# An encoder block on one core: later row sums in the first block, reordered attention work, one sum of the down projection on another engine

## The chip, the cores and the metric

One core of a Trainium2 chip runs the whole kernel. The metric is device time in microseconds of one execution; the median of three runs is given. The core has five engines that work side by side, each with its own in-order queue of instructions: TensorE (PE, with its weight loads PEld), VectorE (DVE), ScalarE (ACT), GpSimd (POOL) and SyncE (SP), which here only starts transfers. They wait for each other by semaphores. SBUF is the on-chip memory of 128 partitions; PSUM has eight banks, into which PE accumulates.

## The reference

One layer of a bidirectional encoder over 512 tokens of width 2048, in float32:

```
h = RMSNorm(x) * g_mix
qA|kA|vA|qB|kB|vB = h @ W_in                  # widths 1024,256,256,1024,1024,1024
A = grouped-query attention, 8 heads of 128 on 2 k/v heads; q, k RMS-normalised per head,
    then 2-D axial rotary (row and column of the token in a grid 64 wide)
B = 8 heads, three dilated windows (128,1),(512,4),(2048,16) merged by their softmax sums;
    partial rotary on the first 32 of 128 dims
x = x + concat(RMSNorm(A), RMSNorm(B)) @ W_out
x = x + (silu(gate) * up) @ W_down,  gate|up = (RMSNorm(x) * g_ffn) @ W_gate_up    # 5632 each
out = RMSNorm(x) * g_final
```

## The kernel before, in words

**Precision.** Every large product is made of three fp32r matmuls (`mm3`, lines 133 to 135): each operand is split into hi (an ACT copy that rounds, `split_hi`, L221 and L223) and lo (DVE: the operand less hi, `split_lo`, L229 and L231), and PE sums hi*hi, hi*lo and lo*hi.

**Units.** The work is a list of units, in the order of PE. A standard unit (`Std`) multiplies 256 rows of a weight by 512 columns in two parts and is planned at 5.44 us (`STD_US`); a wide unit (`Wides`) is one 512-row step of one of seven products (m1 to m7) from which a 2 by 2 block product is put together, planned at 2.72 us (`WIDE_US`). Some of the seven need a sum or difference of weight blocks first: `weights` (L297 for the early blocks, L1072 in down) makes it on DVE, `between` (L1081) makes a second one.

**Order.** Nothing is reordered by a scheduler: the program's order is each engine's order. The loop at the end of the kernel (from L1344) goes through the units; `prepare(n)` starts loads on SP as far ahead as `load_ahead` says, then issues hi splits for up to four units ahead (8.2 us for wide units, 11 for standard ones) and lo splits one unit behind the hi splits. Weights live in a few buffers that are free again when hi and lo are made; the split pairs live in four buffers (`twin`). Functions that `hook(n, f)` leaves with unit n are issued after its matmuls. Two side lists (`side` for attention heads, `side2` for rope, tables and K) are emptied a little after every six matmuls of a standard unit (`tick`, `pump`) at `RATE_B`, `RATE_A` and `RATE_2` entries per unit and row block.

**Stages.** Units 0 to 7 make k and v of mixer A. Meanwhile x arrives in column form (`load_pair`), is scaled by its gain (`x_scale`, L344), split (`x_hi` L347, `x_lo` L350) and summed for the seven products (`x_sums`: L356 and L357 on GpSimd, L360 on DVE, L362 and L364). Rows of x come a second time in row form (`load_rows_in`, L385, through GpSimd's queue) and are squared and summed on ACT (`square_rows`, L388); `make_r1` turns the sums into 1/rms per token, `r1`, after unit 12. Results carry the factor r1 when they leave PSUM: `post_kvA` stores k and v of mixer A, `x_block` the products of three blocks of 28 wide units (v of B; q and k of B twice), in which `snap` copies a product (L463) and `add` adds another to it (L470).

Units 92 to 107 (`qa_chunk`) make q of mixer A and units 108 to 123 (`out_chunk`, kind B) the first half of the output projection. Between their matmuls lies attention: for each head `tq` and `tk` transpose q and k on PE and split them, `score` multiplies and takes the maximum (L685, L681) and the exponential (L687, L682), `weigh` divides by the sum (GpSimd L695, for the last block DVE L693), `pt` transposes and splits the probabilities (L124, L125), `pv` multiplies with v. `fin` splits the result o (hi L127, lo L128), squares it (L724, after the lo) and adds the square to a running sum (GpSimd L733). `push_norm_rope` puts five steps for a row block of q or k on `side2`: squares and 1/rms (`first`, L543), the part with sin on GpSimd (`turned`, L554), the part with cos on DVE (`straight`, L560, in place), their sum (`both`, L563), and the norm (`scaled`, GpSimd L566). `turn_k` transposes K of mixer A.

Then out_chunk A (units 124 to 139) finishes the output projection; `h_side` brings the new x into column form, with its lo halves on DVE (L939). Eleven blocks of 28 wide units make gate and up (`gate_up_block`), and `Down` multiplies by W_down in three passes: m1 with m7 eight units behind it, m6 with m4, m5 with m2, then m3. Each pass goes over 22 pairs of row blocks. In the first, m7 of a pair needs b = c - b (L1072), its hi and lo, and home = b + a (L1081), which m6 reads in the second pass. The left operand comes back from memory in chunks (`chunk`, lo on L1109). `spill_out` adds finished products to memory through GpSimd's queue (L1154).

Of the kernel before, what the change touches and what calls it, by code (L numbers as in the profile page):

```python
# [53 lines left out]
RATE_B, RATE_A, RATE_2 = 3.2, 3.2, 2.6  # L54
# [7 lines left out]
def encoder_block(ctx, tc, x, w_in, g_q_a, g_k_a, w_out, w_gate_up, w_down, g_final,  # L62
# [315 lines left out]
    ROW_AT = ((2, 6, 5), (3, 3, 6), (5, 6, 7), (6, 3, 8), (6, 2, 9), (7, 0, 10), (8, 1, 11), (9, 2, 12))  # L378
    x_rows_in = {}

    def load_rows_in(n):
        t, h = divmod(n, 2)
        at = ROW_AT[n][1]
        x_rows_in[n] = work_at(1024 * at, 1024) if at < 6 else early_a[:, 3].rearrange("p s c -> p (s c)")
        nc.gpsimd.dma_start(x_rows_in[n], x[0, t * P:(t + 1) * P, h * (D // 2):(h + 1) * (D // 2)])  # L385
# [46 lines left out]
    def post_kvA(t, ps):  # L432
        k0 = work_at((0, 512, 2048, 2560)[t], 512)
        nc.scalar.activation(k0, ps[t], AF.Copy, scale=r1["r"][:, t:t + 1])
# [3 lines left out]
    KV_UNITS = in_chunk(1024, lambda t, ps: hook(KP + 4, lambda: post_kvA(t, ps)), None)  # L438
# [6 lines left out]
    def x_block(lo0, lo1, dst0, dst1, late=0):  # L445
# [12 lines left out]
        def snap(form, half, name):  # L458
            def go():
                turns["stage"] += 1  # L460
                d = st[name] = stage[turns["stage"] % 3]
                for t in range(2):
                    nc.scalar.activation(d[:, t], box.bank_of(form)[t], AF.Copy, scale=r(half, t))  # L463
            return go

        def add(form, half, name):
            def go():
                d = st[name]
                for t in range(2):
                    nc.vector.scalar_tensor_tensor(d[:, t], box.bank_of(form)[t], r(half, t), d[:, t],  # L470
                                                   op0=OP.mult, op1=OP.add)
            return go

        def store(dst, half, name):
            return lambda: nc.gpsimd.dma_start(dst[:, 2 * half:2 * half + 2], st[name])
        box.after("m1", late, snap("m1", 0, "c11"))
        box.after("m7", 0, snap("m7", 1, "c22"))
        box.after("m6", 0, snap("m6", 1, "c21"))
        box.after("m2", 1, add("m2", 0, "c11"))
        box.after("m2", 2, store(dst0, 0, "c11"))  # L480
        box.after("m5", 1, add("m5", 1, "c22"))
        box.after("m5", 2, store(dst1, 1, "c22"))
        box.after("m4", 1, add("m4", 1, "c21"))
        box.after("m4", 2, store(dst0, 1, "c21"))
# [50 lines left out]
    def push_norm_rope(q0, dst, t, nh, name):  # L535
# [23 lines left out]
        def straight():  # L559
            nc.vector.tensor_tensor(q3, q3, tabs[name][0][:, t, :][:, None, :].to_broadcast([P, nh, HD]), op=OP.mult)  # L560

        def both():
            nc.vector.tensor_tensor(q0, q0, st["tmp"][:, :w], op=OP.add)  # L563
# [4 lines left out]
        side2.extend((first, turned, straight, both, scaled))  # L568
# [4 lines left out]
    def load_kvA():  # L573
        kvr["t"] = slot("kvr", F32, (P, NT, 512))
        nc.sync.dma_start(kvr["t"], kv_dram)

    kv_split = once("kvs", [P, 8, 512], F32R)

    def push_kvA():
# [12 lines left out]
        side2.append(split_v)  # L592
        kvr["turn"] = [lambda: turn_k(0), lambda: turn_k(1)]
# [3 lines left out]
    def post_qA(j, t, ps):  # L597
# [6 lines left out]
        if j == 0 and t == NT - 1:  # L604
# [844 lines left out]
```

## Time and profile before

| | us |
|---|---|
| median of 3 runs | 2001.19 (2000.93 to 2002.81) |
| the profiled execution | 2002.41 |
| its span, first to last instruction | 2000.6 |
| PE busy | 1971.6 |
| DVE busy | 1490.2 |
| ACT busy | 990.7 |
| POOL busy | 204.0 |
| mean granted clock of PE | 0.997 of full speed |

The span is what the profiler records of the program itself; the execution's time has some 2 us around it. A busy time is the union of an engine's instructions. Matmuls follow each other faster than each one lasts, so PE can be busy without a gap and still not be at its peak. The granted clock is a share of the full 2.4 GHz; 0.50 is 1.2 GHz.

### The profile page before, as it was taken

The page shows a single profiled execution, that of the slowest core. Times are in us where ns is not written, and L with a number is a line of the kernel's source. Part 1 is how long each engine was busy: PE and PEld are TensorE (multiplying, and loading weights), DVE is VectorE, ACT ScalarE, POOL GpSimd, SP SyncE. Part 2 cuts the span into 40 slices and gives each one's busy share as a digit, 9 for nine tenths or more (in the row PEclk, how much of TensorE's full clock was granted, in tenths as well). Part 3 has the DMA queues.
Part 4 walks back from the last instruction along what each step waited for, and adds up shares of the span by engine and source line. Part 5 has one row for each costly group of instructions (what it writes and reads, how often), then busy time and mean ns, then how long its engine had stood idle before and what let it go on. Part 6 is the DMA issues. An engine that isn't in the chain of part 4 may idle for free.

```text
span 2000.6 us, 23772 instructions
## 1 busy us (share of the span) xinstructions
PE 1971.6 (99%) x8932; PEld 1619.6 (81%) x8932; DVE 1490.2 (74%) x1731; ACT 990.7 (50%) x1262; POOL 204.0 (10%) x237
## 2 busy tenths in 40 slices
PE   9999999999999999999999999999999999999998
PEld 6788888777888888888888888888888887888886
DVE  6777666776654687777777877787778799788776
ACT  7644435554544554454444544444544545455464
POOL 3100014654220000000000000000000001002000
PEclk9999999999999999999999999999999999999999
DMA  6785684242334656657558567466475997479855
GB/s 234 256 278 178 202 275 140 95 136 76 129 103 150 228 171 230 216 165 265 177 199 271 174 218 259 159 230 229 156 264 190 341 363 233 161 243 339 284 179 176
DMA packets 219092, 418.67 MB, mean 209 GB/s; under 512 B 13664, under 2 KB 40032, under 8 KB 218720
## 3 DMA queue, kind: packets, MB, share of 16 engines
q1 hardware_dynamic: 210176, 389.86, 58.2%
q0 software_dynamic: 8656, 27.27, 4.4%
q8 instruction: 70, 1.15, 0.2%
q14 instruction: 46, 0.38, 0.1%
q10 hardware_dynamic: 144, 0.02, 0.0%
HBM read 369.65 MB, written 47.45 MB: 208 GB/s over the span
## 4 chain that ended last, share of the span: by engine, by line
PE 64%; DVE 2%; DMA 1%; issue 1%; ACT 1%; ACTq 0%; POOLq 0%; SPq 0%; POOL 0%; DVEq 0%
PE zc L133 8%; PE zc L135 8%; PE zc L134 8%; PE yc L134 4%; PE yc L135 4%; PE yc L133 4%; PE zd L134 4%; PE zd L135 4%; PE zd L133 4%; PE yd L135 3%; PE yd L133 3%; PE yd L134 3%; PE xc L133 2%; PE xc L134 2%; PE xc L135 2%; PE at L1005 1%
## 5 line engine op out<-in xcount | busy, mean ns | idle before, releaser
L231 DVE TENSOR_TENSOR twin<-whole,twin 128x1024 fp32r<-128x1024 f32 x172 | 214.1, 1246 | 101.6 <-ACT twin L223 101.3
L223 ACT ACTIVATE twin<-st1b 128x1024 fp32r<-128x1024 f32 x172 | 182.7, 1062 | 193.8 <-PE zc L135 66.5
L133 PE MATMUL zc<-twin,arena 128*128 128x512 f32 x704 | 277.1, 394 | 0.0
L135 PE MATMUL zc<-twin,arena 128*128 128x512 f32 x704 | 274.5, 390 | 0.0
L134 PE MATMUL zc<-twin,arena 128*128 128x512 f32 x704 | 274.1, 389 | 0.0
L223 ACT ACTIVATE twin<-whole 128x1024 fp32r<-128x1024 f32 x172 | 181.8, 1057 | 155.3 <-PE yc L135 74.0
L231 DVE TENSOR_TENSOR twin<-st1b,twin 128x1024 fp32r<-128x1024 f32 x172 | 209.9, 1221 | 33.2 <-ACT twin L223 32.6
L223 ACT ACTIVATE twin<-st1a 128x1024 fp32r<-128x1024 f32 x128 | 135.8, 1062 | 184.7 <-PE xc L135 58.2
L231 DVE TENSOR_TENSOR twin<-st1a,twin 128x1024 fp32r<-128x1024 f32 x128 | 156.4, 1223 | 69.9 <-ACT twin L223 64.9
L135 PEld LDWEIGHTS zc<-twin,arena 128*128 128x128 f32 x704 | 132.1, 188 | 28.1
L133 PEld LDWEIGHTS zc<-twin,arena 128*128 128x128 f32 x704 | 132.2, 188 | 27.0
L134 PEld LDWEIGHTS zc<-twin,arena 128*128 128x128 f32 x704 | 132.3, 188 | 26.3
L134 PE MATMUL yc<-twin,arena 128*128 128x512 f32 x352 | 137.2, 390 | 0.7 <-DVE twin L231 0.7
L133 PE MATMUL yc<-twin,arena 128*128 128x512 f32 x352 | 137.9, 392 | 0.0
L135 PE MATMUL yc<-twin,arena 128*128 128x512 f32 x352 | 137.1, 389 | 0.0
L134 PE MATMUL zd<-twin,form 128*128 128x512 f32 x348 | 135.5, 389 | 0.1
L133 PE MATMUL zd<-twin,form 128*128 128x512 f32 x348 | 135.6, 390 | 0.0
L135 PE MATMUL zd<-twin,form 128*128 128x512 f32 x348 | 135.4, 389 | 0.0
L1154 POOL DMA_DIRECT2D x1d<-ev x16 | 14.0, 873 | 1073.5 <-ACT ev L1153 1058.9
L134 PE MATMUL yd<-twin,form 128*128 128x512 f32 (+1 forms) x272 | 105.3, 387 | 1.6 <-DVE twin L231 1.6
L135 PE MATMUL yd<-twin,form 128*128 128x512 f32 (+1 forms) x272 | 105.1, 386 | 0.1
L133 PE MATMUL yd<-twin,form 128*128 128x512 f32 (+1 forms) x272 | 105.0, 386 | 0.0
(285 smaller groups left out, 4355.8 us busy)
## 6 DMA issues: line engine op xcount, KB each, us to landing
whole<-in_w_gate_up_dram SPq DMA_DIRECT2D x165, 512.0 KB, 5.1
whole<-in_w_in_dram SPq DMA_DIRECT2D x80, 512.0 KB, 4.6
st<-in_w_gate_up_dram SPq DMA_DIRECT2D x55, 512.0 KB, 3.9
st1a<-in_w_down_dram SPq DMA_DIRECT2D x48, 512.0 KB, 7.0
st1b<-in_w_down_dram SPq DMA_DIRECT2D x48, 512.0 KB, 8.5
st1a<-in_w_gate_up_dram SPq DMA_DIRECT2D x44, 512.0 KB, 7.3
st1b<-in_w_gate_up_dram SPq DMA_DIRECT2D x44, 512.0 KB, 6.5
forms<-pair SPq DMA_DIRECT2D x22, 896.0 KB, 6.7
```

The lines of the kernel that those rows point to most:

```text
L133: nc.tensor.matmul(dst, ah, bh, start=start, stop=False, skip_group_check=chained)
L134: nc.tensor.matmul(dst, ah, bl, start=False, stop=False, skip_group_check=chained)
L135: nc.tensor.matmul(dst, al, bh, start=False, stop=stop, skip_group_check=chained)
L223: nc.scalar.activation(self.pair[:, :, 0], self.src, AF.Copy)
L231: nc.vector.tensor_tensor(self.pair[:, :, 1], self.src, f32(self.pair[:, :, 0]), op=OP.subtract)
L1005: nc.tensor.transpose(ps[:, n * P:(n + 1) * P], src, ident)
L1154: nc.gpsimd.dma_start(x1_dram[2 * cb + j, row], e, accum_op=OP.add)
```

## The change

Four groups of edits:

- The rows of x are loaded after units 7 to 20 in place of 2 to 9, and squared at units 10 to 23 in place of 5 to 12; r1 is there from unit 23 on. `post_kvA` stores k and v without the factor, after units 8 to 11; `scale_kvA` applies it on ACT when they come back. The V block copies and adds its products without the factor and scales them on ACT ahead of the store (`store`), at later units. In units 0 to 7, and where the rate is 1.5 (out_chunk A), the lo splits are issued as far ahead as the hi splits. In units 0 and 1 `x_scale` comes ahead of a part of `prepare`.
- In `fin` the square of o is issued between hi and lo.
- The rope's part with cos is written to a buffer of its own ("rc"), with an empty step ahead of the sum; `RATE_2` goes from 2.6 to 3.2; the two `turn_k` come right after the rope of k.
- home = b + a (`between`), and in the last two steps of `h_side` the lo half of three forms, go from DVE to GpSimd.

```diff
--- before.py
+++ after.py
@@ -51,7 +51,7 @@
 CHUNK = 4
 ORDER = ("m1", "m4", "m5", "m3", "m2", "m7", "m6")
 X_AT = {"m1": (0, 1), "m4": (0, 2), "m2": (0, 3), "m5": (1, 0), "m6": (1, 1), "m7": (1, 2), "m3": (1, 3)}
-RATE_B, RATE_A, RATE_2 = 3.2, 3.2, 2.6
+RATE_B, RATE_A, RATE_2 = 3.2, 3.2, 3.2
 
 
 def f32(ap):
@@ -375,13 +375,11 @@
         return w[:, 0, lo:lo + P], w[:, 1, lo:lo + P]
 
     r1 = {}
-    ROW_AT = ((2, 6, 5), (3, 3, 6), (5, 6, 7), (6, 3, 8), (6, 2, 9), (7, 0, 10), (8, 1, 11), (9, 2, 12))
+    ROW_AT = ((7, 2, 10), (10, 2, 13), (13, 2, 16), (14, 0, 17), (16, 2, 19), (17, 0, 20), (19, 2, 22), (20, 0, 23))
     x_rows_in = {}
-
     def load_rows_in(n):
         t, h = divmod(n, 2)
-        at = ROW_AT[n][1]
-        x_rows_in[n] = work_at(1024 * at, 1024) if at < 6 else early_a[:, 3].rearrange("p s c -> p (s c)")
+        x_rows_in[n] = work_at(1024 * ROW_AT[n][1], 1024)
         nc.gpsimd.dma_start(x_rows_in[n], x[0, t * P:(t + 1) * P, h * (D // 2):(h + 1) * (D // 2)])
 
     def square_rows(n):
@@ -430,12 +428,12 @@
         return std_chunk(w_in, 0, lo, KP, mm, group, **kw)
 
     def post_kvA(t, ps):
-        k0 = work_at((0, 512, 2048, 2560)[t], 512)
-        nc.scalar.activation(k0, ps[t], AF.Copy, scale=r1["r"][:, t:t + 1])
+        k0 = work_at((1024, 1536, 0, 512)[t], 512)
+        nc.scalar.activation(k0, ps[t], AF.Copy)
         nc.gpsimd.dma_start(kv_dram[:, t], k0)
 
     QB, KB, VB = 1536, 2560, 3584
-    KV_UNITS = in_chunk(1024, lambda t, ps: hook(KP + 4, lambda: post_kvA(t, ps)), None)
+    KV_UNITS = in_chunk(1024, lambda t, ps: hook(KP + t, lambda: post_kvA(t, ps)), None)
     KV_UNITS[0].quick = KV_UNITS[0].raws[0].halves = True
     for n, u in enumerate(KV_UNITS):
         u.load_ahead = 20.0
@@ -460,28 +458,39 @@
                 turns["stage"] += 1
                 d = st[name] = stage[turns["stage"] % 3]
                 for t in range(2):
-                    nc.scalar.activation(d[:, t], box.bank_of(form)[t], AF.Copy, scale=r(half, t))
+                    if late and form != "m3":
+                        nc.scalar.activation(d[:, t], box.bank_of(form)[t], AF.Copy)
+                    else:
+                        nc.scalar.activation(d[:, t], box.bank_of(form)[t], AF.Copy, scale=r(half, t))
             return go
 
         def add(form, half, name):
             def go():
                 d = st[name]
                 for t in range(2):
-                    nc.vector.scalar_tensor_tensor(d[:, t], box.bank_of(form)[t], r(half, t), d[:, t],
-                                                   op0=OP.mult, op1=OP.add)
+                    if late:
+                        nc.vector.tensor_tensor(d[:, t], box.bank_of(form)[t], d[:, t], op=OP.add)
+                    else:
+                        nc.vector.scalar_tensor_tensor(d[:, t], box.bank_of(form)[t], r(half, t), d[:, t],
+                                                       op0=OP.mult, op1=OP.add)
             return go
 
         def store(dst, half, name):
-            return lambda: nc.gpsimd.dma_start(dst[:, 2 * half:2 * half + 2], st[name])
-        box.after("m1", late, snap("m1", 0, "c11"))
-        box.after("m7", 0, snap("m7", 1, "c22"))
-        box.after("m6", 0, snap("m6", 1, "c21"))
+            def go():
+                if late and name != "c12":
+                    for t in range(2):
+                        nc.scalar.activation(st[name][:, t], st[name][:, t], AF.Copy, scale=r(half, t))
+                nc.gpsimd.dma_start(dst[:, 2 * half:2 * half + 2], st[name])
+            return go
+        box.after("m1", 2 * late, snap("m1", 0, "c11"))
+        box.after("m7", 8 * late, snap("m7", 1, "c22"))
+        box.after("m6", 3 * late, snap("m6", 1, "c21"))
         box.after("m2", 1, add("m2", 0, "c11"))
-        box.after("m2", 2, store(dst0, 0, "c11"))
+        box.after("m2", 2 + late, store(dst0, 0, "c11"))
         box.after("m5", 1, add("m5", 1, "c22"))
-        box.after("m5", 2, store(dst1, 1, "c22"))
+        box.after("m5", 2 + late, store(dst1, 1, "c22"))
         box.after("m4", 1, add("m4", 1, "c21"))
-        box.after("m4", 2, store(dst0, 1, "c21"))
+        box.after("m4", 2 + late, store(dst0, 1, "c21"))
         box.after("m3", 0, snap("m3", 0, "c12"))
         box.after("m3", 1, store(dst1, 0, "c12"))
         return box
@@ -557,15 +566,17 @@
         q3 = q0.rearrange("p (h d) -> p h d", h=nh)
 
         def straight():
-            nc.vector.tensor_tensor(q3, q3, tabs[name][0][:, t, :][:, None, :].to_broadcast([P, nh, HD]), op=OP.mult)
+            st["cos"] = slot("rc")
+            c3 = st["cos"][:, :w].rearrange("p (h d) -> p h d", h=nh)
+            nc.vector.tensor_tensor(c3, q3, tabs[name][0][:, t, :][:, None, :].to_broadcast([P, nh, HD]), op=OP.mult)
 
         def both():
-            nc.vector.tensor_tensor(q0, q0, st["tmp"][:, :w], op=OP.add)
+            nc.vector.tensor_tensor(q0, st["cos"][:, :w], st["tmp"][:, :w], op=OP.add)
 
         def scaled():
             nc.gpsimd.tensor_tensor(dst.rearrange("p (h d) -> p h d", h=nh), q3,
                                     st["rs"][:, :, None].to_broadcast([P, nh, HD]), op=OP.mult)
-        side2.extend((first, turned, straight, both, scaled))
+        side2.extend((first, turned, straight, lambda: None, both, scaled))
 
     qA, kTA, vA = {}, {}, {}
     kvr = {}
@@ -573,6 +584,9 @@
     def load_kvA():
         kvr["t"] = slot("kvr", F32, (P, NT, 512))
         nc.sync.dma_start(kvr["t"], kv_dram)
+
+    def scale_kvA(t):
+        nc.scalar.activation(kvr["t"][:, t], kvr["t"][:, t], AF.Copy, scale=r1["r"][:, t:t + 1])
 
     kv_split = once("kvs", [P, 8, 512], F32R)
 
@@ -589,8 +603,7 @@
         def split_v():
             vA["v"] = split(kvr["t"][:, :, 256:], "vA", None, [kv_split[:, 4 + 2 * n:6 + 2 * n].rearrange(
                 "p a (b c) -> p (a b) c", b=2) for n in range(2)])
-        side2.append(split_v)
-        kvr["turn"] = [lambda: turn_k(0), lambda: turn_k(1)]
+        side2.extend((lambda: None, lambda: turn_k(0), split_v, lambda: turn_k(1)))
 
     q_rows = {}
 
@@ -601,8 +614,6 @@
         nc.scalar.activation(q0, ps[t], AF.Copy, scale=r1["r"][:, t:t + 1])
         push_norm_rope(q0, q0, t, 4, "q")
         side2.append(lambda: qA.__setitem__((j, t), q0))
-        if j == 0 and t == NT - 1:
-            side2.extend(kvr["turn"])
 
     pairB = {}
 
@@ -719,9 +730,10 @@
             sq = slot("sq") if self.h else misc[:, 2 + "BA".index(self.kind)]
             if last:
                 nc.scalar.activation(sq, self.o, AF.Square)
-            split(self.o, "oS", go[:, k:k + 1], (o[:, 0], o[:, 1]))
+            nc.scalar.activation(o[:, 0], self.o, AF.Copy, scale=go[:, k:k + 1])
             if not last:
                 nc.scalar.activation(sq, self.o, AF.Square)
+            nc.vector.scalar_tensor_tensor(o[:, 1], self.o, go[:, k:k + 1], f32(o[:, 0]), op0=OP.mult, op1=OP.subtract)
             if spill:
                 nc.gpsimd.dma_start(o_dram[self.h], o)
                 spilled.add(self.h)
@@ -801,6 +813,8 @@
     hook(n + 2, load_tables)
     hook(n + 3, push_tables)
     hook(n + 4, load_kvA)
+    for t in range(NT):
+        hook(n + 5 + t // 2, lambda t=t: scale_kvA(t))
     hook(n + 6, push_kvA)
     qa_chunk(1)
 
@@ -936,7 +950,7 @@
                 if half == 2:
                     nc.scalar.activation(hi, src, AF.Copy)
                 if half == 3 or not apart:
-                    nc.vector.tensor_tensor(lo, src, f32(hi), op=OP.subtract)
+                    (nc.gpsimd if apart and a else nc.vector).tensor_tensor(lo, src, f32(hi), op=OP.subtract)
         if half == (3 if apart else 2):
             hf[i] = True
 
@@ -1078,7 +1092,7 @@
         def between(self, form, q):
             if form == "m7":
                 a = self.home[q].t
-                nc.vector.tensor_tensor(a, self.raws[form, q]["b"].t, a, op=OP.add)
+                nc.gpsimd.tensor_tensor(a, self.raws[form, q]["b"].t, a, op=OP.add)
 
         def chunks(self):
             uses = {}
@@ -1292,17 +1306,17 @@
                     raw.load()
             done["load"] += 1
 
-    def prepare(n):
+    def prepare(n, most=4):
         load_raws(n)
         while done["side"] < len(units) and at[done["side"]] <= at[n] + SIDE_AHEAD:
             for v in units[done["side"]].side_in:
                 v.load()
             done["side"] += 1
-        while done["hi"] < min(len(units), n + 4) and at[done["hi"]] <= at[n] + units[done["hi"]].ahead:
+        while done["hi"] < min(len(units), n + most) and at[done["hi"]] <= at[n] + units[done["hi"]].ahead:
             load_raws(n)
             units[done["hi"]].split_hi()
             done["hi"] += 1
-            while done["lo"] < done["hi"] - 1:
+            while done["lo"] < done["hi"] - (n >= KP and units[n].rate != 1.5):
                 units[done["lo"]].split_lo()
                 done["lo"] += 1
         while done["lo"] <= n:
@@ -1358,14 +1372,17 @@
                 x_lo(n + 1)
             if 0 < n < KP - 2:
                 load_pair(n + 2)
-        for k, (first, _, at_unit) in enumerate(ROW_AT):
+        for k, (_, _, at_unit) in enumerate(ROW_AT):
             if n == at_unit:
                 square_rows(k)
         if n == ROW_AT[-1][2]:
             make_r1()
+        if n == 0:
+            prepare(n, 2)
+            x_scale(0)
+        elif n == 1:
+            x_scale(1)
         prepare(n)
-        if n < 2:
-            x_scale(n)
         for j in range(u.parts):
             u.mm(j)
             if j == 0 and n < KP:
```

## Rows read from the trace of the kernel before

**Rows 1.** What PE waited for, whole span: us in total, times, longest.
```profile
PE pj L134 <- DVE twin L231: 4.5, 4, 2.6
PE sc L133 <- DVE pTl L125: 4.4, 6, 1.7
PE o L133 <- ACT p L682: 1.7, 1, 1.7
PE sc L133 <- DVE xrows L855: 1.7, 1, 1.7
...
PE yc L134 <- DVE twin L231: 0.7, 1, 0.7
...
PE pw L134 <- DVE twin L231: 0.4, 1, 0.4
```

**Rows 2.** Windows by stage: length, then busy us of PE, PEld, DVE, ACT, POOL.
```profile
5.39:58.60 53.21, 48.72 (x192) 38.56 (x193) 38.13 (x37) 39.78 (x51) 21.67 (x23) 0.97 0.73 259
58.60:310.00 251.40, 251.40 (x1122) 208.09 (x1122) 178.59 (x174) 119.76 (x137) 25.82 (x37) 1.00 0.69 229
310.00:502.00 192.00, 181.50 (x882) 143.81 (x881) 135.90 (x327) 93.34 (x178) 97.41 (x110) 0.99 0.34 110
...
630.00:740.00 110.00, 108.71 (x507) 88.87 (x506) 76.57 (x98) 61.93 (x94) 1.92 (x1) 1.00 0.55 188
...
1584.90:1686.50 101.60, 99.93 (x438) 81.56 (x436) 99.65 (x90) 49.41 (x52) 3.55 (x4) 1.00 0.91 316
```

**Rows 3.** Windows of low clock; the seventh figure is PE's granted clock.
```profile
51.50:54.92 3.42, 3.04 (x7) 2.46 (x8) 3.42 (x4) 2.77 (x4) 1.44 (x2) 0.50 1.01 393
...
454.28:457.69 3.41, 3.41 (x11) 2.83 (x10) 2.26 (x4) 2.25 (x5) 2.10 (x2) 0.50 0.03 7
```

**Rows 4.** Line L388, squares of rows: ns min/median/max, first and last start.
```profile
L388 ACT ACTIVATE early_work<-early_work x6: 1041/1043/1061, 46.2 to 69.7; 128x1024 f32<-128x1024 f32 x6
```

**Rows 5.** Line L385, loads of rows, from issue to landing.
```profile
DMA to landing us min/median/max: 4.3/5.2/7.5
```

**Rows 6.** What ACT waited for at L724, 310 to 502 us.
```profile
ACT sq L724 <- DVE oS L128: 11.1, 5, 3.4
...
ACT misc L724 <- DVE oS L128: 2.0, 1, 2.0
```

**Rows 7.** What DVE waited for at L560, 310 to 502 us.
```profile
DVE qA L560 <- POOL ra L554: 10.7, 6, 2.6
...
DVE kvr L560 <- POOL ra L554: 2.9, 2, 1.8
```

**Rows 8.** Line L939, lo halves of the forms, 630 to 740 us.
```profile
L939 DVE TENSOR_TENSOR arena<-pair,arena x16: 949/1085/1227, 642.8 to 728.3; 128x1024 fp32r<-128x1024 f32 x8, 128x768 fp32r<-128x768 f32 x8
```

**Rows 9.** Line L1081 (22 in all): ns min/median/max, first and last start.
```profile
L1081 DVE TENSOR_TENSOR home<-st1a,home x8: 1219/1220/1222, 1588.3 to 1675.9; 128x1024 f32<-128x1024 f32 x8
```

**Rows 10.** Time line of DVE near 1680 us: start, duration.
```profile
1679.97 1.22 DVE L1081 TENSOR_TENSOR home<-st1b,home 128x1024 f32<-128x1024 f32 x1
1681.11 1.22 DVE L231 TENSOR_TENSOR twin<-st1b,twin 128x1024 fp32r<-128x1024 f32 x1
```

**Rows 11.** Time line of PE there; in brackets the idle time before.
```profile
1682.38 0.50 PE L134 MATMUL yd<-twin,form 128*128 128x512 f32 x1 [1.02 <-DVE twin L231]
```

**Rows 12.** Time line of DVE, 49 to 54 us.
```profile
49.47 0.68 DVE L360 TENSOR_TENSOR early_work<-early_work 128x512 f32<-128x512 f32 x1
50.08 1.75 DVE L231 TENSOR_TENSOR twin<-whole,twin 128x1024 fp32r<-128x1024 f32 x1
```

**Rows 13.** Time line of POOL, 49 to 54 us.
```profile
49.64 1.10 POOL L356 TENSOR_TENSOR early_work<-early_work 128x256 f32<-128x256 f32 x1 [0.42 <-DVE xsum L364]
50.82 1.59 POOL L357 TENSOR_TENSOR early_work<-early_work 128x256 f32<-128x256 f32 x1
```

**Rows 14.** Time line of DVE, 343 to 346 us.
```profile
343.15 1.22 DVE L231 TENSOR_TENSOR twin<-whole,twin 128x1024 fp32r<-128x1024 f32 x1
```

**Rows 15.** Time line of POOL, 343 to 346 us.
```profile
344.24 1.31 POOL L733 TENSOR_TENSOR misc<-misc,sq 128x512 f32<-128x512 f32 x1
```

## The prediction

> **What bounds the kernel now.** I read the list of what TensorE (PE) waited for first, then the busy times by stage, and only then the lists and time lines of the engines that feed it. The reader should see in [rows 1] that every large wait of PE is for VectorE (DVE) or ScalarE (ACT), none for a transfer, and in [rows 2] that the waits lie in four stretches. The rest is full: from 58.6 to 310 us PE is busy 251.40 of 251.40. The first block of the input projection idles 53.21 - 48.72 = 4.5 us, attention 192.00 - 181.50 = 10.5, the end of the output projection 110.00 - 108.71 = 1.3, the first pass of down 101.60 - 99.93 = 1.7. No matmul is added or taken away, so only these idle times, and new ones, can move the end. Twice an idle spell is followed by about 3.4 us at the lower clock, 0.50 [rows 3]: behind the stall at 49 us and behind that at 451 us. PE was busy there 3.04 of 3.42 and 3.41 of 3.41 us, at half pace, so about 1.7 us is lost each time. That makes 4.5 + 1.7 = 6.2 us to be had in the first block and 10.5 + 1.7 = 12.2 in attention.
>
> **The first block and the rows of x.** Eight squares of 1.04 us [rows 4] leave ACT in units 5 to 12, with their eight half-megabyte loads on GpSimd's queue, and the lo halves are issued a unit earlier on DVE. PE's four waits there, 4.5 us, are all for a lo (L231) [rows 1], which stands on DVE behind the lo of x, and that behind ACT. One unit earlier is 5.44 us in the plan (STD_US), twice the longest wait, 2.6. I take all 6.2 us. The squares land in units 10 to 23, inside the stretch where PE is full and ACT busy 119.76 of 251.40 [rows 2]. Each load has about three units (3 x 2.72 = 8.2 us) less the unit by which ACT runs ahead, 5.4 us at least, and landed in 4.3 to 7.5 us [rows 5]. A late one stops ACT for up to 2 us, behind it the hi halves of weights that are three units ahead: hidden, and if that cover went, 8 x 2 = 16 us. The four k/v stores and the three stores of the V block wait on the same queue and feed nothing before attention. The scaling moved behind r1 adds six ACT passes over 128x512 in the same full stretch; half of a 1.04 us pass each up to a whole one, 3 to 6 us on an engine with 130 us free: nothing.
>
> **Attention.** The square of o reads the PSUM bank that DVE's lo reads, and today it waits for that lo: ACT stood 11.1 + 2.0 us and two smaller times for it [rows 6], with the next hi of the probabilities behind it in ACT's queue. Ahead of the lo it waits for nothing, and the lo is up to 0.6 us later. The rope in place makes DVE's product with cos wait for GpSimd, which still reads the same q: 10.7 + 2.9 us [rows 7], with scores' maxima and lo halves queued behind. Out of place, only the sum needs GpSimd, three entries of the side list later instead of one. Side entries come 3.2/2.6 = 1.23 times as fast, but a rope has six instead of five: the same pace, nothing. The scores that waited for lo halves (4.4 us), for the maximum through the exponential (1.7) and for the residual row (1.7), and the low clock behind the second (1.7), are what late DVE work costs: 9.5 of 12.2. New are four ACT passes that scale k and v (2 to 4 us by the 1.04 of [rows 4], on an engine busy 93.34 of 192.00), for half a microsecond; and both K transposes come 2 entries behind the last GpSimd product that they read, where they came behind four more ropes. I take 9 us, between 0 (late work that only moves) and 12.2.
>
> **The output projection.** With the lo not held back, the 0.4 us wait at pw goes [rows 1]. But at its end two lo halves of 128x768 (0.95 us on DVE [rows 8]) go to GpSimd; by the working below they hold DVE 1.8 us, and the second stands just ahead of the 0.7 us wait at yc: +0.8. Together +0.4.
>
> **One sum of down on GpSimd.** The additions home = b + a (L1081) of 22 pairs, 1.22 us on DVE [rows 9], go to GpSimd. In the tail DVE starts an operation every 1681.11 - 1679.97 = 1.14 us [rows 10], and that is what it gets back for each. DVE is the engine with no room there: busy 99.65 of 101.60 [rows 2], and PE waited 1.02 us for its lo at 1682.38 [rows 11]. So whatever these operations do to DVE reaches the end one for one, and giving 22 x 1.14 = 25 us away sounds right. The trace speaks against it. At 49 us GpSimd adds beside DVE, and the two take turns: DVE's L360 ends at 49.47 + 0.68 = 50.15, GpSimd's L356, issued at 49.64, ends at 50.74, 0.59 after it; DVE's L231, issued at 50.08, ends at 51.83, 1.09 after that; GpSimd's L357, issued at 50.82, ends at 52.41, 0.58 after that [rows 12, 13]. DVE's operation took 1.75 instead of 1.22. So 128x256 holds DVE for 0.58 us. For 128x512: DVE's L231 ends at 343.15 + 1.22 = 344.37 [rows 14], L733, issued 344.24, at 345.55 [rows 15]: 1.18. The slope is 0.60 per 256 columns, so 128x1024, which no row shows, holds 0.58 + 3 x 0.60 = 2.38 us. DVE in down runs only operations with two inputs in SBUF, the kind that lost its turn at 50 us. Each moved sum thus costs 2.38 - 1.14 = 1.24 us in place of a gain: 22 x 1.24 = 27.3, less DVE's idle time 101.60 - 99.65 = 2.0, less the last sum's 2.4, whose end PE need not await: +23 us. Bounds: with no turns DVE has 25 us spare and the 1.7 us of waits vanish, -1.7; with two 128x512 additions whole, 2 x 1.31 = 2.62, it is 22 x 1.48 - 2 = +31. I take the row, because the operations on both sides are of its kind. PE would stand nearly half of the last nine units, and may see the low clock; since it then waits for DVE anyway I add nothing.
>
> The Trainium skill, SBUF — State Buffer, section "Who interferes with whom", says that a DVE instruction with two SBUF inputs and a GpSimd instruction that reads SBUF block each other for the whole instruction. The trace agrees, with 1.75 us for 1.22. The GPSIMD Engine Reference of the Trainium skill, "Elementwise — side-by-side cycle accounting", gives 4497 ns for an addition of 2048 columns; half, an estimate of 2.25 us, would make 22 x 1.11 - 4.4 = +20, and no row here shows it.
>
> **The sum.** The profiled execution took 2002.41 us (span 2000.6 and 1.8 around it), 1.2 above the median of 2001.19. 2002.4 - 6.2 - 9 + 0.4 + 23 = 2010.6; less the 1.2, 2009.4, and I say 2009.
>
> **Rivals.** *The sum hides beside DVE.* GpSimd then works in time in which DVE is not using the shared path, DVE drops to three quarters, the waits of down go: 2001.2 - 6.2 - 9 + 0.4 - 1.7 = 1985, faster. For it: GpSimd is idle through down but for a few issues (3.55 us [rows 2]). Against it: DVE has only 2 us without such an operation, and every overlap I followed took turns. It decides where the hold falls below 1.14 + (14.8 + 4.4)/22 = 2.0 us. Perfetto Trace Analysis of the Trainium skill, "Optimizing Scalar/DVE Operations", holds that with DVE saturated moving work, even to GpSimd, may make sense, and warns of the shared port for that pair; the first half is this rival, and the trace bears out the warning.
> *The gains balance the loss.* Attention gives all 12.2 and the sum costs 18, where GpSimd finds DVE waiting oftener than at 50 us: 2001.2 - 6.2 - 12.2 + 0.4 + 18 = 2001, no change. For it: most waits in [rows 1] have one of the two removed causes behind them. Against it: a late DVE has shown other reasons in attention, among them the same turns with GpSimd.
> *Attention only moves its waits.* The K transposes stop PE for GpSimd's product, the new ACT passes delay the next hi, and the 9 us stay: 2018, slower still. For it: two entries are about 3 us of PE's time and GpSimd has the weighting of the probabilities in the same queue. Against it: 13.6 us of DVE's waiting [rows 7] are really gone.
>
> **Chances and range.** The forecast has 0.55, its own range 2003 to 2016; the hidden sum 0.15; the balance 0.16; the moved waits 0.14. 0.2% is 4 us, about what a measurement of this kernel can tell from no change. Faster, below 1997, is the hidden sum and a little of the balance: 0.17. Same: most of the balance and the lower end of the forecast: 0.18. Slower: 0.65. The range for 8 in 10 runs from 1991, which leaves out most of the hidden sum, to 2018, which leaves out half of the moved waits.
>
> **What would show it.** Right: PE without waits before 58 us and no low clock there; first pass of down about 124 us long instead of 102, with L231 and L1072 near 1.2 and 2.4 to 3.6 us by turns and GpSimd's additions at 2.4 or more; PE waiting there for L231 above all, over 20 us. L560 and L724 no longer behind GpSimd and DVE. Wrong: DVE at 1.22 us beside GpSimd's additions, or PE in down without new waits (the term of 23 us falls); ACT waiting for rows of x between 70 and 100 us; PE waiting at kt.

## The result and the profile after

The changed kernel takes 2010.09 us (median of 5 runs, 2009.34 to 2010.60), the kernel before, in the same comparison, 2000.98: a ratio of 1.0046, interval 1.0031 to 1.0060. So the change costs 9 us, which the predicted 2009 came close to. The profiled execution has a span of 2008.5 us against 2000.6, +7.9.

What PE waited for, whole span (us in total, times, longest), beside [rows 1]:

```profile
PE yd L134 <- DVE twin L231: 9.9, 5, 4.6
PE zd L135 <- DVE form L1123: 5.2, 3, 2.4
PE yd L135 <- DVE form L1123: 2.9, 2, 2.3
PE pt L711 <- DVE pTl L125: 2.2, 2, 1.1
...
PE yc L134 <- DVE twin L231: 1.1, 1, 1.1
...
PE zc L135 <- DVE arena L953: 0.4, 1, 0.4
...
PE sc L133 <- DVE pTl L125: 0.3, 1, 0.3
PE kt L600 <- POOL kvr L577: 0.3, 1, 0.3
```

What is left of DVE's wait behind GpSimd's part of the rope, 302 to 484 us, beside [rows 7]:

```profile
DVE qA L574 <- POOL ra L563: 0.6, 1, 0.6
```

The 4.5 us at pj are gone and the score waits of 4.4 us are down to 0.3. DVE's waits, 13.6 us in [rows 7], are 0.6, and ACT no longer waits for lo at the square [rows 6] (1.9 us are left there, put down to the rope's sum). In their place stand three rows of down, 18.0 us in all. L1123 is the lo half of the left operand's chunks, L1109 before. The busy times by stage (length, then PE, PEld, DVE, ACT, POOL, granted clock), at the stages' new places, beside [rows 2]; the last two rows are shorter windows, two of the places where the clock fell:

```profile
5.39:51.00 45.61, 45.61 (x193) 37.59 (x194) 38.02 (x36) 35.78 (x43) 18.51 (x17) 1.00 0.71 258
51.00:302.40 251.40, 251.40 (x1122) 207.99 (x1121) 179.44 (x177) 126.39 (x151) 29.11 (x43) 1.00 0.72 237
302.40:483.50 181.10, 177.12 (x882) 143.39 (x881) 141.38 (x331) 96.70 (x185) 102.19 (x112) 1.00 0.36 118
...
611.50:722.30 110.80, 109.01 (x507) 88.81 (x506) 77.03 (x95) 61.74 (x94) 6.75 (x3) 1.00 0.54 186
...
1567.70:1694.40 126.70, 108.75 (x441) 85.80 (x440) 125.74 (x70) 48.95 (x52) 71.31 (x26) 0.92 0.77 254
...
1668.00:1682.00 14.00, 8.67 (x19) 6.16 (x20) 14.00 (x7) 2.21 (x3) 9.73 (x5) 0.52 0.88 254
1691.50:1696.00 4.50, 3.10 (x8) 2.47 (x9) 4.50 (x4) 1.46 (x2) 0.80 (x1) 0.62 0.46 138
```

The first block has no idle time and full clock; attention is 181.1 us long instead of 192.0; the first pass of down is 126.7 instead of 101.6, with 20 DVE instructions fewer (70 in place of 90) and DVE busy 26 us longer. Where that comes from is plain on the time lines of DVE and POOL in the tail of that pass, where [rows 10] had an operation every 1.14 us:

```profile
1650.35 1.21 DVE L231 TENSOR_TENSOR twin<-home,twin 128x1024 fp32r<-128x1024 f32 x1
1651.49 3.41 DVE L1086 TENSOR_TENSOR st1b<-st1b,st1b 128x1024 f32<-128x1024 f32 x1
1654.82 1.21 DVE L231 TENSOR_TENSOR twin<-st1b,twin 128x1024 fp32r<-128x1024 f32 x1
1655.96 3.41 DVE L1086 TENSOR_TENSOR whole<-whole 128x1024 f32<-128x1024 f32 x1
...
1650.56 3.25 POOL L1095 TENSOR_TENSOR home<-st1b,home 128x1024 f32<-128x1024 f32 x1 [4.09 <-DVE st1b L1086]
1655.03 3.25 POOL L1095 TENSOR_TENSOR home<-st1b,home 128x1024 f32<-128x1024 f32 x1 [1.22 <-issue]
```

GpSimd's addition, issued at 1650.56, stands until DVE's running operation has ended at 1651.56, then runs to 1653.81; DVE's next, issued at 1651.49, ends only at 1654.90. A sum on GpSimd thus holds DVE for 3.41 - 1.21 = 2.20 us.

All kernels issue the same 7908 matmuls outside attention, in the same order. The start of the same matmul, less its start in the profiled execution before, gives how far each kernel is ahead (negative) or behind at a place. The experiments are in the same table:

| start before, us: | 58.65 first V product | 113.05 V block | 620.12 behind attention | 743.55 gate and up | 1579.85 down | 1787.59 second pass |
|---|---|---|---|---|---|---|
| the change | -7.7 | -7.6 | -18.5 | -17.7 | -17.2 | +7.9 |
| e1_sum_back | -8.1 | -7.2 | -18.1 | -17.3 | -17.1 | -17.7 |
| e2_both_back | -7.7 | -7.6 | -18.4 | -19.2 | -18.9 | -19.5 |
| e3_sum_alone | -1.4 | -1.4 | -1.4 | -1.5 | -1.2 | +21.7 |
| e4_sum_twice | -2.2 | -0.4 | -1.7 | -1.7 | -1.5 | +54.1 |
| e11_spare_sum | -2.5 | -1.1 | -2.5 | -2.6 | -2.2 | +42.6 |
| e10_half_sum | -8.6 | -8.5 | -19.4 | -20.2 | -19.9 | -8.3 |
| e5_square_alone | -1.5 | -1.3 | -1.8 | -1.8 | -1.6 | -2.2 |
| e6_rope_alone | -0.6 | +0.7 | -8.5 | -8.5 | -8.3 | -8.6 |
| e12_rope_buffer | -3.2 | -1.8 | +0.9 | +0.8 | +1.2 | +0.6 |
| e7_square_rope | -2.9 | -0.9 | -13.0 | -13.1 | -12.8 | -13.5 |
| e8_lo_ahead | -7.2 | -1.3 | -1.3 | -2.1 | -1.9 | -2.5 |
| e9_rows_moved | -5.5 | -5.3 | -16.3 | -16.3 | -16.0 | -16.6 |

Kernels whose first 113 us are those of before stand there between +0.7 and -1.8, on average at -0.8: single executions differ that much, and the one profiled before was a late one.

### The profile page after: what moved, and what is told of

Same layout as the page of the kernel before. It is cut to its first block, busy times and chain, and to the rows that moved or that the text cites. A ratio compares the mean times of both kernels' runs of the same rounds, so it can differ in the third digit from the quotient of the medians.

```text
span 2008.5 us, 23826 instructions
## 1 busy us (share of the span) xinstructions
PE 1973.7 (98%) x8932; PEld 1622.4 (81%) x8932; DVE 1520.8 (76%) x1707; ACT 994.2 (49%) x1272; POOL 278.3 (14%) x261
## 4 chain that ended last, share of the span: by engine, by line
PE 89%; DVE 5%; issue 4%; ACT 2%; DMA 1%; POOL 0%; SPq 0%; ACTq 0%; POOLq 0%; DVEq 0%
PE zc L135 10%; PE zc L133 10%; PE zc L134 10%; PE yc L134 5%; PE yc L135 5%; PE yc L133 5%; PE zd L134 3%; PE zd L135 3%; PE zd L133 3%; PE pw L133 3%; PE pw L135 3%; PE pw L134 3%; PE xc L133 2%; PE xc L134 2%; PE xc L135 2%
## 5 line engine op out<-in xcount | busy, mean ns | idle before, releaser
L231 DVE TENSOR_TENSOR twin<-whole,twin 128x1024 fp32r<-128x1024 f32 x172 | 220.8, 1285 | 110.5 <-ACT twin L223 108.1
L231 DVE TENSOR_TENSOR twin<-st1b,twin 128x1024 fp32r<-128x1024 f32 x172 | 216.0, 1256 | 33.4 <-ACT twin L223 32.7
L231 DVE TENSOR_TENSOR twin<-st1a,twin 128x1024 fp32r<-128x1024 f32 x128 | 171.7, 1342 | 70.0 <-ACT twin L223 60.4
L1095 POOL TENSOR_TENSOR home<-st1a,home 128x1024 f32<-128x1024 f32 x8 | 24.5, 3102 | 869.4 <-DMA forms<-pair 855.3
L134 PE MATMUL yd<-twin,form 128*128 128x512 f32 (+1 forms) x272 | 108.0, 397 | 9.9 <-DVE twin L231 9.9
L135 PE MATMUL yd<-twin,form 128*128 128x512 f32 (+1 forms) x272 | 107.5, 395 | 2.9 <-DVE form L1123 2.9
L133 PE MATMUL yd<-twin,form 128*128 128x512 f32 (+1 forms) x272 | 107.2, 394 | 0.0
```

The lines of the kernel that those rows point to most:

```text
L133: nc.tensor.matmul(dst, ah, bh, start=start, stop=False, skip_group_check=chained)
L134: nc.tensor.matmul(dst, ah, bl, start=False, stop=False, skip_group_check=chained)
L135: nc.tensor.matmul(dst, al, bh, start=False, stop=stop, skip_group_check=chained)
L231: nc.vector.tensor_tensor(self.pair[:, :, 1], self.src, f32(self.pair[:, :, 0]), op=OP.subtract)
L1095: nc.gpsimd.tensor_tensor(a, self.raws[form, q]["b"].t, a, op=OP.add)
```

## The experiments

Times are medians; the kernel before ran beside each group on the same chip at 1999.88, 1999.74 and 2000.20 us.

**The sum of down: e1, e3, e11, e4, e10.** The sum back on DVE, the rest as changed:

```
-                nc.gpsimd.tensor_tensor(a, self.raws[form, q]["b"].t, a, op=OP.add)
+                nc.vector.tensor_tensor(a, self.raws[form, q]["b"].t, a, op=OP.add)
```

> The changed kernel with the 22 sums home = b + a back on DVE; everything else as changed. Taking turns (the two engines exclude each other, and that is all the loss of down): the first pass of down gets back the 25.5 us that it lost, DVE's operations there are 1.22 us each again, PE waits there about 1.7 us: 2010.1 - 25.5 = 1984.6, between 1982 and 1988. Rival, other cause (the pass is late because it now begins 17.7 us sooner in memory traffic, or since the clock falls): it stays above 2000.

1984.29 us, ratio 0.9920 (0.9906 to 0.9933). PE waits 0.9 us in that pass. The whole loss of down is this one line. The reverse, that line alone in the kernel before:

> The kernel before with only the 22 sums home = b + a on GpSimd. Taking turns: down loses the same as in the changed kernel, 2001.0 + 25.5 = 2026.5, between 2022 and 2030; DVE's operations there are 1.22 or 3.4 us. Rival, the sum hides and the loss belongs to the changed attention: 1999 to 2001.

2025.54 us, ratio 1.0126 (1.0113 to 1.0140). The loss doesn't depend on the other edits. These two don't yet say whether DVE is held or whether home and b come free too late. For that GpSimd gets work that relieves nobody and that nobody needs, first badly placed:

```
                 nc.vector.tensor_tensor(a, self.raws[form, q]["b"].t, a, op=OP.add)
+                b = self.raws[form, q]["b"].t
+                nc.gpsimd.tensor_tensor(b, b, a, op=OP.add)
```

> The kernel before, with DVE making home = b + a as before and GpSimd adding b = b + a after it, a result that nothing reads: work is added, none is taken away. Taking turns: each GpSimd addition holds DVE for 2.2 us, 22 x 2.2 = 48.4, less the 2.0 us that DVE had idle there: about 2047, between 2040 and 2050. Rival, late buffers (the loss in the changed kernel comes from home and b being free later, not from DVE): the same buffers are held as long, so 2026 as with the sum alone. Rival, nothing holds DVE: 2001.

2058.28 us, above everything expected. `between` is issued ahead of L231 of the same b, so the lo half is made from the overwritten b (m7 is another product in this kernel), and it waits for GpSimd by a semaphore. The trace shows it: no DVE operation there is longer than 1.23 us, but L231 waits 51.0 us, 20 times, for the new line. The experiment added a dependence and tells nothing of the hold. The same into c, whose content is used up by then:

```
+                r = self.raws[form, q]
+                nc.gpsimd.tensor_tensor(r["c"].t, r["b"].t, a, op=OP.add)
```

> The kernel before, DVE making home = b + a as before, and GpSimd adding c = b + home after it, into a buffer whose content is used up: 22 additions that nothing waits for but a later load, and no DVE work is taken away. The output is unchanged. Taking turns: each addition holds DVE for the 2.15 us that the 20 long DVE operations of the changed kernel show, 22 x 2.15 = 47, less 2.0 idle: about 2045, between 2040 and 2049, and DVE's operations show 3.4 us. Rival, nothing holds DVE, and the kernel with the sum written into b was late only since the lo half waited for it: 2000 to 2004.

2046.38 us, ratio 1.0228 (1.0214 to 1.0242). Its time line of DVE and POOL:

```profile
1645.71 1.21 DVE L231 TENSOR_TENSOR twin<-st1b,twin 128x1024 fp32r<-128x1024 f32 x1
1646.84 3.38 DVE L1111 TENSOR_TENSOR form<-form_raw,form 128x1024 fp32r<-128x1024 f32 x1
1650.15 1.21 DVE L1072 TENSOR_TENSOR st1b<-whole,st1b 128x1024 f32<-128x1024 f32 x1
...
1645.86 3.28 POOL L1083 TENSOR_TENSOR st1b<-st1b,home 128x1024 f32<-128x1024 f32 x1 [4.57 <-DVE home L1081]
```

Each of the 22 additions has its long DVE operation here, up to 3.42 us, and together these last 47.7 us more than 1.21 each: 2.17 us per addition. At the second pass 44.8 of them have reached PE (from -2.2 to +42.6). Whichever DVE operation comes next is hit, here the lo half of a chunk, which has nothing to do with the sum. That the two engines hold each other up is shown (GpSimd's addition takes 3.28 us here, and 2.35 to 2.40 in e4, where DVE waits); late buffers aren't needed for it. Half of the columns, with the lo halves of the forms (L953) on DVE as in e2 below:

```
-                nc.gpsimd.tensor_tensor(a, self.raws[form, q]["b"].t, a, op=OP.add)
+                b = self.raws[form, q]["b"].t
+                nc.vector.tensor_tensor(a[:, 0], b[:, 0], a[:, 0], op=OP.add)
+                nc.gpsimd.tensor_tensor(a[:, 1], b[:, 1], a[:, 1], op=OP.add)
```

> The changed kernel with the lo halves of the forms on DVE and each sum of down cut in two: the first half of the columns (128x512) on DVE, the second on GpSimd. Taking turns, hold in proportion to the columns: 2.15 / 2 = 1.08 held, 0.62 of DVE's own half, against 1.14 for the whole: 22 x 0.56 = 12 us above the 1982.9 of the kernel with both moves undone: 1995. Rival, the short addition fits between DVE's operations: 1983 or below.

1994.84 us, 12.0 above the 1982.87 of e2. A half of 128x512 on DVE itself lasts 0.68 us, and 1.78 when it is held, 1.10 more:

```profile
1602.54 1.78 DVE L1096 TENSOR_TENSOR home<-st1a,home 128x512 f32<-128x512 f32 x1
...
1601.61 2.16 POOL L1097 TENSOR_TENSOR home<-st1a,home 128x512 f32<-128x512 f32 x1 [2.95 <-DVE st1a L1086]
```

The hold goes with the columns, 0.55 us per 256 at both sizes (1.10 / 2, 2.20 / 4).

**The lo halves of the forms: e2.** L953 back on DVE as well:

> The changed kernel with the sums of down and the lo halves of the forms at the end of the output projection back on DVE. Taking turns: the 1.5 us that PE lost at the end of the output projection come down to the 0.7 of before, so 0.8 us below the kernel with only the sums back, about 1983.8, and the wait for L953 there is gone. Rival (these two halves cost DVE nothing): the same time as that kernel within 0.3 us.

1982.87 us, ratio 0.9914 (0.9901 to 0.9928), 1.4 below e1; their runs overlap, but the table has the same: across the output projection e1 falls back by 0.8 and e2 gains 0.8. This is the fastest kernel of the study, 17 us below the one before. In the changed kernel the second moved half stood beside DVE's own lo half of the forms:

```profile
708.66 2.86 DVE L953 TENSOR_TENSOR arena<-pair,arena 128x1024 fp32r<-128x1024 f32 x1
...
707.68 2.75 POOL L953 TENSOR_TENSOR arena<-pair,arena 128x768 fp32r<-128x768 f32 x1 [9.50 <-DVE st1b L297]
```

2.86 - 1.22 = 1.64 us of hold, 0.55 per 256 columns again, for an operation that DVE does in 0.95.

**Attention: e5, e6, e7, e12.** The square ahead of lo, alone:

```
-            split(self.o, "oS", go[:, k:k + 1], (o[:, 0], o[:, 1]))
+            nc.scalar.activation(o[:, 0], self.o, AF.Copy, scale=go[:, k:k + 1])
             if not last:
                 nc.scalar.activation(sq, self.o, AF.Square)
+            nc.vector.scalar_tensor_tensor(o[:, 1], self.o, go[:, k:k + 1], f32(o[:, 0]), op0=OP.mult, op1=OP.subtract)
```

> The kernel before with only the square of o issued ahead of its lo. If each wait belongs to its own cause: ACT's 17 us of waiting at the square go, and the part of PE's 10.9 us gain in attention that hangs on ACT with them, some 4 us: 1997. Rival, late work only moves to the next wait (the rope): less than 1.5 us, 2000. Rival, the square is the whole cause: 1990.

2000.23 us, ratio 1.0002 (0.9993 to 1.0011): nothing. ACT's waits at the square for lo are gone, and it waits 10.2 us longer for the maximum ahead of the exponential, 50.4 us where the kernel before had 40.2:

```profile
ACT p L687 <- DVE whole L685: 50.4, 23, 6.1
```

The rope, alone, with all of its edits (buffer "rc", empty step, `RATE_2` 3.2, K transposes):

> The kernel before with only the rope's edits (the part with cos into a buffer of its own, the empty step, the rate of 3.2, the two K transposes after the rope of k). If each wait belongs to its own cause: DVE's 13.6 us of waiting behind GpSimd go, and PE gains some 6 us: 1995. Rival, only moved: 2000. Rival, the rope is the whole cause: 1990.

1991.68 us, ratio 0.9958 (0.9944 to 0.9971). Both:

> The kernel before with both the square ahead of lo and the rope's edits. The two together are all that attention gained in the changed kernel, 10.9 us: 1990, between 1988.5 and 1991.5. If it is clearly less, the early start of attention after a shorter first block or the scaling of k and v moved there has a share. If the two alone add up to this, the causes are separate; if they add up to more, each removes part of the same waits.

1989.35 us, ratio 0.9944 (0.9932 to 0.9957). The two alone give 8, together 10.4: the square is worth nothing by itself and 2.3 us once the rope is changed. While DVE is late for GpSimd's sake, ACT has only to wait elsewhere. Then the rope's buffer and its empty step alone, in the kernel before; the rate of 2.6 and the place of the K transposes stay as they were:

```
+            st["cos"] = slot("rc")
...
-        side2.extend((first, turned, straight, both, scaled))
+        side2.extend((first, turned, straight, lambda: None, both, scaled))
```

> The kernel before with the rope's part with cos in a buffer of its own and the empty step ahead of the sum, but the rate of 2.6 and the place of the K transposes as before. If DVE's wait behind GpSimd's product is what held attention: nearly all of what all rope edits gave, 8 us: 1992. Rival, the rate and the earlier K transposes gave it: under 3 us, 1997 to 2000.

2002.97 us, ratio 1.0013 (1.0004 to 1.0022). DVE's wait behind L554 is down to 2.3 us, once, yet nothing is won. What PE waited for from 300 to 510 us:

```profile
PE qt L661 <- POOL qA L568: 6.7, 1, 6.7
PE sc L133 <- DVE pTl L125: 2.8, 5, 0.7
```

One wait of 6.7 us, at 442 us, for the norm of the last rows of q, the last entry of a rope; and the clock stands at 0.50 for 6.8 us around it. Six entries in place of five at the old rate bring the list in late: the whole of that last rope, from its squares (L543, 435.1 us) on, runs while PE waits. What the buffer saved is lost there. In e6 the same wait is 0.8 us. The late K transposes stand behind this wait (442.1 us) and can't be its cause, but no run raises the rate alone.

**The first block: e8, e9.** Only the lo halves ahead:

```
-            while done["lo"] < done["hi"] - 1:
+            while done["lo"] < done["hi"] - (n >= KP and units[n].rate != 1.5):
```

> The kernel before with only the line that issues the lo halves as far ahead as the hi halves in units 0 to 7 (and in the second half of the output projection). Squares and loads of rows stay where they were. If the lo was late because it was issued late: the first block gives most of its 7.6 us, 0.7 more in the output projection: 1993 to 1994. Rival, the lo was late because the squares and the split of x kept ACT and DVE from it: under 2 us, 1999 to 2001, and PE still waits for L231 there.

1999.53 us, ratio 0.9997 (0.9988 to 1.0006). The table shows what neither theory had: 7.2 us ahead at the first V product, 1.3 at 113 us. What PE, and then DVE, waited for in that stretch:

```profile
PE yc L134 <- DVE twin L231: 2.3, 1, 2.3
PE zc L134 <- DVE twin L231: 1.3, 1, 1.3
...
DVE early_work L297 <- DMA early_work<-in_w_in_dram: 3.2, 2, 3.0
DVE st0b L297 <- DMA st0b<-in_w_in_dram: 1.7, 1, 1.7
```

Its busy times from 60 to 70 us (the second last figure is the DMA engines' share):

```profile
60.00:70.00 10.00, 6.35 (x23) 4.81 (x23) 5.99 (x6) 5.98 (x8) 0.00 (x0) 0.88 1.01 365
```

And line L206, weights issued from 49 to 56 us, until landing:

```profile
DMA to landing us min/median/max: 4.4/10.7/12.5
```

PE gets to the wide units sooner, and the weight differences (L297) wait for weights. Full DMA engines are the smaller part of that: in the changed kernel, with a share of 0.93 in the same ten us, a like set of weights lands in 8.6 us (median) instead of 10.7. But it is issued ten us sooner, from 39 to 44 us. What kept SP from issuing it in e8, 36 to 62 us:

```profile
SPq L206 <- ACT early_a L388: 9.1, 1, 9.1
```

In the kernel before, two of the eight loads of rows go into a weight buffer (the fourth of `early_a`). SP, whose queue is in order, can't load weights there until ACT has squared the rows, and all later weights stand behind that load. The kernel before has the same wait, 5.4 us, but there PE comes to these weights 7 us later. The changed kernel puts the rows elsewhere, and the wait is gone. The other half, the rows (and all that goes with them) moved and lo not ahead, both moves to GpSimd undone:

> The changed kernel with both GpSimd moves undone, and with the lo halves of units 0 to 7 (and of the second half of the output projection) issued one unit behind the hi halves again, as before; loads and squares of the rows of x stay at their later units. If the late lo is what holds PE: its four waits come back, 1982.9 + 6 + 0.7 = 1989.6. If the loads and squares of the rows are, and the lo ahead matters little: 1982.9 + 2 at 20 and 26 us + 0.7 = 1985.6 or less.

1986.08 us, ratio 0.9928 (0.9915 to 0.9940), 3.2 above e2. That is near the 1985.6 expected, but by another wait than expected there. Of the four waits in the kernel before (20, 26, 43 and 52 us) two are left, 0.2 us of the one at 26 and 1.6 of the 2.6 us of the one at 52, which stands at 48 us here:

```profile
PE pj L134 <- DVE twin L231: 1.7, 2, 1.6
...
47.84 0.50 PE L134 MATMUL pj<-twin,xbase 128*128 128x512 f32 x1 [1.55 <-DVE twin L231]
```

The granted clock stays at 1.00 behind it.

So, counted from the average of -0.8 at 113 us, the lo ahead alone gives 0.5 us, which the spread there hides, the rows alone 4.5, and both 6.9 (the four kernels with both stand at -7.7 on average).

## Why the prediction was right

The time was right, and so was what decides it: GpSimd's sums hold DVE longer than DVE needs for them. That it was right to 1 us is luck in part: the gains came out 3.3 us larger than forecast (by the table 1.4 in the first block, 1.9 in attention) and the losses 2.5 (0.4 and 2.1). Term by term, from the table:

- **First block, -6.2.** Measured -7.6 in the pair of profiles, -6.9 against the average of executions. The size holds; the reason given, that one unit earlier on DVE is enough, was half of it. The lo halves alone bring the first V product forward and lose it again to late weights (e8). What keeps the gain, by e8's trace, is that no rows stand in a weight buffer any more, for which SP waited 9.1 us; I had weighed the loads only for being late themselves, not for what stands behind their buffer in SP's queue. No run moves those two loads alone. With the rows moved and lo not ahead, the waits at 20 and 43 us go and the one at 52 us is shorter (e9).
- **Attention, -9.** Measured -10.9, within the bounds of 0 and 12.2. The step on the rope was right about the cause and right that rate and step belong together ("the same pace, nothing"): without the rate, PE waits 6.7 us (e12). The step on the square was too generous: 17 us of ACT's waiting were worth 0 alone and 2.3 behind the rope. The two together give 12.1 without the first block's edits (e7) and 10.8 to 11.0 with them. Those last 1.2 us may be nothing: among kernels whose attention is as before, single executions differ by 1.4 us in that stretch (0.0 in e3, -1.4 in e11).
- **Output projection, +0.4.** Measured +0.8. The wait at pw went (-0.7); the moved halves cost 1.5, not 0.8. The hold of 1.8 us was right (1.64).
- **Down, +23.** Measured +25.1. The hold was mis-sized, 2.38 us where 2.20 was measured, and so was what I took off. I had counted how long GpSimd ran past DVE's last operation (0.58 us for 256 columns), not what DVE lost by it, which stood in the same row: 1.75 - 1.22 = 0.53, and four times that is 2.12. From the first L1072 or L1086 of the pass to the last lo half of a chunk that PE waits for, DVE took 101.4 us before and takes 125.2, +23.7: 22 holds of 2.20 less 21 sums of 1.14 (the last one of before came after that), less 1.0 of DVE's idle time (not 2.0), 23.5. The last addition was not free of charge, since that lo half stands behind it. Then 1.4 more: from PE's last wait to the second pass it is 6.46 us instead of 5.10, the clock being at 0.50 behind that wait. I had named that clock and added nothing for it. The errors in these sizes partly cancelled.
- **The rivals.** The sum that hides needed a hold under 2.0 us; it was 2.20, not far above. The GPSIMD Engine Reference of the Trainium skill, section "Elementwise — side-by-side cycle accounting", gave an estimated 2.25 us, and the measured 2.20 is nearer to that than to my 2.38. "Attention only moves its waits" fell: only 4.0 us of idle time are left there, and PE at kt waits 0.3. "The gains balance the loss" was right for attention alone.

Of the signs named ahead, first block, L231 and L1086 at 1.2 or 3.4 us, GpSimd at 2.4 us or more and the missing waits at the rope and the square all came. One did not: over 20 us of waiting for L231. It is 9.9 for L231 in that pass, and 8.1 for the chunks' lo half: PE waits for whichever operation was held. Of the signs of being wrong one came, but small: PE's wait at kt, 0.3 us.

## What to carry to other kernels

Before work is moved from DVE to GpSimd, ask what it holds there, not what it relieves: here an addition of two SBUF operands costs DVE 2.20 us in GpSimd's hands and 1.14 in its own. Where data is parked in a buffer that other loads use, look at which loads stand behind it in the queue (9.1 us of SP here), and where steps are added to a paced list, raise the pace with them. And try the parts one by one: this change was 27 us of loss in two lines over 17 us of gain, and the gain alone (1982.87) is the better kernel.

## What the runs showed of the hardware

GpSimd doesn't always give the way back to DVE after each addition. In the changed kernel two of its sums had been dammed up behind accumulating stores and a third was just ready; they ran in one go, 2.35 us apart, and a DVE operation issued before the first stood 8.61 us. PE then waited 4.6 us, the longest wait of the run:

```profile
1670.26 8.61 DVE L231 TENSOR_TENSOR twin<-st1a,twin 128x1024 fp32r<-128x1024 f32 x1
...
1670.47 2.70 POOL L1095 TENSOR_TENSOR home<-whole,home 128x1024 f32<-128x1024 f32 x1
1672.82 4.96 POOL L1095 TENSOR_TENSOR home<-st1a,home 128x1024 f32<-128x1024 f32 x2
```

That is (8.61 - 1.21) / 3 = 2.47 us for each, so a row of them is no dearer per sum than single ones by much, but its whole price falls on one operation. It need not come so: in e3 the same three sums were dammed up at the same place, and the two engines took turns one by one:

```profile
1687.41 3.41 DVE L1072 TENSOR_TENSOR st1b<-st1b,st1b 128x1024 f32<-128x1024 f32 x1
1690.75 3.40 DVE L231 TENSOR_TENSOR twin<-st1a,twin 128x1024 fp32r<-128x1024 f32 x1
1694.08 3.41 DVE L1072 TENSOR_TENSOR st1b<-whole,st1b 128x1024 f32<-128x1024 f32 x1
...
1687.02 2.71 POOL L1081 TENSOR_TENSOR home<-whole,home 128x1024 f32<-128x1024 f32 x1
1689.69 6.71 POOL L1081 TENSOR_TENSOR home<-st1a,home 128x1024 f32<-128x1024 f32 x2
```

What decides between the two is not shown. The Trainium skill, SBUF — State Buffer, section "Who interferes with whom", has the engine that issues first hold the shared path for its whole instruction. Single sums agree with it: GpSimd's was issued at 1650.56, DVE's next operation at 1651.49, and DVE stood. The three in one go do not, by the starts recorded: DVE's operation, issued 0.21 us before the first of them, stood through all three.
